# New places for operands and a second order of products in one feed-forward product of a two-layer encoder

## The chip, the cores and the metric

The kernel runs on one core of a Trainium2 chip. The metric is device time in microseconds (us) from the first to the last instruction of the program on the slowest core, here the only one. A core has five engines that run side by side: TensorE multiplies matrices (PE in the profile; PEld is its loading of the stationary operand), VectorE (DVE), ScalarE (ACT) and GpSimd (POOL) work elementwise, SyncE (SP) starts transfers. Tiles lie in SBUF, 128 partitions wide; products are summed in PSUM, eight banks of 512 float32 a partition.

## The reference

Two layers act on 272 tokens (16 learned meta tokens and 256 others) of width 2048. Each layer projects the tokens once, runs two groups of attention heads on the result (a gated linear attention in both directions, and a neighbourhood attention over a grid), joins them by an output projection, and then applies a feed-forward block of width 8192. After both, the residual stream is normalised. What the change touches is the second product of the feed-forward block:

```python
    ff = jnp.einsum('blf,fd->bld', jnp.square(jax.nn.relu(jnp.einsum('bld,df->blf', h, w_ff1))), w_ff2)
    return _layer_norm(DEEPNORM_ALPHA * h + ff, ln2_w, ln2_b)
```

The inner product and the squared ReLU give 272 x 8192 activations, which the kernel calls u; w_ff2 is 8192 x 2048. All is float32.

## The kernel before

**Split operands.** Every float32 operand is held as two rounded parts, a high and a low one (dtype float32r), and a product is the sum of three: high weights by high activations (h), high weights by low activations (l), low weights by high activations (w). The weights' parts are made on the chip: a block of 128 x 1024 weights is fetched into a tile `raw`, ScalarE rounds it to `wh` (L275, `rest`) and VectorE forms `wl = raw - wh` (L277). `made` does this one block after another in the order that the generator `order` yields, three blocks ahead of TensorE; four buffers each of `wh` and `wl`, 1280 floats wide, are in rotation, three of `raw`.

**Places.** A block of 1024 weights is eight blocks of 128, stored in pairs. `blocks`, `block` and `pairs` place them in the 1280 floats by three numbers, in floats: where the first block begins, the step from the first block of a pair to the second, the step from one pair to the next. The tables HIGHS and LOWS give these for each kind of block; for the stage of the change the kind is "all":

```python
"all": (0, P, 2 * P)                # HIGHS, P = 128
"all": (0, P + 16, 2 * P + 64)      # LOWS
```

Activations lie in chunks of 128 features by 272 tokens. `pair` makes one: a tile of 2 x 288 floats, the high part in the first 288, the low part in the second, so 1152 bytes apart and 2304 bytes in all. The inputs of a product are 16 such chunks (x, y), or 32 (y and u).

**Layer one's feed-forward block** (`tail`, with l = 0) goes over the 8192 features in two halves of 4096, that is 32 chunks: 16 take the tiles of y, which are free by then, and 16 are in a pool of their own, u. In each half the first product (w_ff1) writes the 32 chunks, and the second product (w_ff2) sums over them into the accumulator `acc` of 16 output chunks of 128 features each. The second product is `by_m`, called for groups g = 0 to 3 of four outputs m = 0 to 3: for each output, four groups of eight chunks (y 0 to 7, y 8 to 15, u 16 to 23, u 24 to 31), and for each group one call of `weights` and one of `eight`.

**`eight`** (L311) issues the 24 matmuls of a group into one PSUM bank: weights stationary (128 x 128), activations moving (128 x 272). Their order is a string, where each letter counts up its own chunks:

```python
TURNS = {True: "hwhwhwhwhwhwhwhw", False: "hlhlwwhlhlwwhlhlwwhlhlww"}
```

The second string is used where the moving operand is 272 wide. Each matmul loads its stationary operand anew. After each group `pump` lets a piece of other work be issued where some is waiting (in this stage hardly any; in half 1 the pieces of the layer norm), and after the last group of an output `ev_2` adds the bank to `acc` (L991, or `ln_part` in half 1). No planner is at work: the order of instructions is the order of the program, on each engine's own queue; the semaphores between engines are placed by the framework.

By the same line L311 run layer one's other by-output products; L363 is the same in another order of loops (`by_k`, the first product of a layer), L323 and L1184 are layer two's products, which have 256 tokens.

Of the kernel before, what the change touches and what calls it, by code (L numbers as in the profile page):

```python
# [8 lines left out]
F32R = mybir.dt.float32r  # L9
# [5 lines left out]
P = 128  # L15
D = 2048
DC = D // P
T = 256
NM = 16
L = T + NM  # L20
# [27 lines left out]
HIGHS = {"flat": (16, P, 2 * P), "once": (0, P, 2 * P), "two": (0, P, 2 * P), "all": (0, P, 2 * P), "all2": (0, P, 2 * P), "own2": (0, P + 48, 2 * P + 64)}  # L48
LOWS = {"flat": (16, P, 2 * P), "once": (16, P + 32, 2 * P + 64), "two": (16, P + 16, 2 * P + 64), "all": (0, P + 16, 2 * P + 64),
        "all2": (0, P + 48, 2 * P + 64), "own2": (0, P + 32, 2 * P + 64)}  # L50
TURNS = {True: "hwhwhwhwhwhwhwhw", False: "hlhlwwhlhlwwhlhlwwhlhlww"}


def plan(half, g):

    n, last = FEWER[half][g], HELD if half and g == 3 else 0
    special = list(range(FIRST, FIRST + n))
    plain = [k for k in range(DC) if k not in special]
    out = [(plain.pop(0), "flat")]
    for i, k in enumerate(special):  # L60
        out += [(k, "quad"), (plain.pop(0), "flat"), (k, "sums")]
        more = (i + 1) * (DC - 2 * n - 2 - last) // n - i * (DC - 2 * n - 2 - last) // n
        out += [(plain.pop(0), "flat") for _ in range(more)]
    return out + [(k, "flat") for k in plain]
# [13 lines left out]
class Trunk:  # L78
# [93 lines left out]
    def order(self):  # L172

        i, first = self.i, [(), (WB // 2, WB)]
        for l in range(DEPTH):
            last = l + 1 == DEPTH
            kind = lambda short, name: name if last and short else "all"
            na = [kind(c % 3 == 0, "two") for c in range(24)]
            groups = [(i["win"][l, g], [kind(g in (3, 4, 5), "two")] * 4 if g < 6 else na[4 * g - 24:4 * g - 20]) for g in range(12)]
            if last:  # L180
                groups[0] = groups[0][0], ["all2"] * 4
            groups += [(i["wout"][l, g], [kind(True, "once")] * 4) for g in range(4)]
            for half in range(2):
                groups += [(i["wff1"][l, 8 * half + g], [kind(True, "once") if half or g > 1 else ("all2", "own2")[last]] * 4)
                           for g in range(8)]
                groups += [(i["wff2"][l, half, g], plan(half, g) if last else ["all"] * 4) for g in range(4)]
            if l == 0:
                for t in range(groups[0][0].shape[0]):
                    for w, _ in groups[:2]:
                        yield w[t], first.pop(0) if first else (WB,), "all"  # L190
                groups = groups[2:]
            for w, kinds in groups:
                n = w.shape[0]
                if n == DC and last and isinstance(kinds[0], tuple):
                    for t, kind in kinds:
                        yield w[t], (WB,), kind
                    continue
                for t in range(n):
                    yield w[t], (WB,), kinds[4 * t // n]
# [94 lines left out]
        for at in (slice(4, 6), slice(6, 8)):  # L294
            self.halves(raw[:, at.start * P:at.stop * P], wh, wl, at)

    def eight(self, ps, wh, wl, x, n, first, last, once):

        mm = self.nc.tensor.matmul
        seen = dict.fromkeys("hlw", 0)
        for i, kind in enumerate(TURNS[once]):
            j = seen[kind]
            seen[kind] += 1
            w, v, o = wl if kind == "w" else wh, x[j], ps[:, :n]
            rhs = v[kind == "l"][:, :n]
            if once:
                rhs, o = (v.once, ps) if kind == "h" else (v[0][:, :T], ps[:, T:])  # L310
            mm(o, lhsT=self.block(w, j), rhs=rhs, start=first and not i, stop=last and i == len(TURNS[once]) - 1)  # L311

    def sixteen(self, ps, x, first, last, pump):

# [58 lines left out]
                self.nc.tensor.matmul(o, lhsT=self.block(both[low], i), rhs=rhs, start=not low and k + i % 2 == 0,  # L373
                                      stop=k == DC - 2 and i % 2 == 1 and not low, skip_group_check=True)

    def by_m(self, acts, ns, evict, pump=(0, 0), apart=False, renew=False, slim=()):

        nk = len(acts)
        for m, n in enumerate(ns):
            once = n == T and m not in slim  # L380
            ps = self.pm.tile([P, 512], F32, name="mm", tag="mm")
            step = 16 if once and acts[0].dense else 8
            for k in range(0, nk, step):
                if step > 8:
                    self.sixteen(ps, acts[k:k + 16], not k, k == nk - 16, pump)
                else:
                    wh, wl = self.weights()
                    self.eight(ps, wh, wl, acts[k:k + 8], n, not k, k == nk - 8, once)
                if k < nk - step:
                    self.pump(*pump)  # L390
                if renew and m == len(ns) - 1 and not k:
                    self.renew(2)
            parts = [ps[:, :T], ps[:, T:]] if once else [ps[:, :n]]
            evict(m, parts if apart else self.whole(parts))
            self.pump(*pump)
# [11 lines left out]
    def pair(self, pool, name, c):  # L407
        both = pool.tile([P, 2, PITCH], F32R, name=f"{name}{c}", tag=f"{name}{c}", bufs=1)
        return Pair(both, dense=name in ("y", "u") and not self.full)


    def layer(self, l):
        nc, tc = self.nc, self.tc
# [524 lines left out]
    def tail(self, ps):  # L938
        nc, tc, l, n = self.nc, self.tc, self.l, self.n
        last = l == DEPTH - 1  # L940
        acc = self.acc
        with tc.tile_pool(name="u", bufs=1, reuse_waits="tile") as up:
# [5 lines left out]
            for g in range(1, 4):  # L948
                self.by_m(self.y, [n] * 4, lambda m, ps: self.ln_part(4 * g + m, 0, ps),
                          pump=(0.75 if last else 1, 0), apart=True)  # L950
            self.fg.append(self.ln_norm(0, l, n))
            for half in range(2):
                u = [self.pair(self.yp, "y", k) if k < DC else self.pair(up, "u", k) for k in range(2 * DC)]
                if last:
                    u = [self.turned(x.both, k % 2) for k, x in enumerate(u)]
                    self.u, self.combined = u, {}
# [17 lines left out]
                for g in range(8):  # L974
                    if half or g > 2:
                        self.by_m(self.x, [n] * 4, lambda m, ps: ev_f(4 * g + m, ps), pump=(1, 0))
                    elif g == 2:
                        ps = self.by_k(self.x, n, self.normed, ends=True)
# [4 lines left out]
                    else:  # L983
                        self.by_m(self.x, [n + 2] * 4, lambda m, ps: self.fixed(ev_f, 4 * g + m, ps),
                                  pump=(1, NORMS[1]), renew=g == 1)

                def ev_2(m, ps, g):
                    k = 4 * g + m
                    a = acc[:, k, :n]
                    if half == 0:  # L990
                        nc.vector.scalar_tensor_tensor(a, a, ALPHA, ps[0], ALU.mult, ALU.add)  # L991
                        for part in ps[1:]:
                            nc.vector.tensor_tensor(a, a, part, ALU.add)
                    else:
                        self.ln_part(k, 1, ps)
# [3 lines left out]
                for g in range(4):  # L999
                    if last:  # L1000
                        self.across(u, half, g)
                    else:
                        self.by_m(u, [n] * 4, lambda m, ps: ev_2(m, ps, g), pump=(1, 0), apart=True)
            if last:
                self.lctx.close()
            else:
# [514 lines left out]
```

## Time and profile before

| | |
|---|---|
| median of 3 runs | 2309.95 us (2308.13 to 2310.82) |
| the profiled execution: time / span | 2308.73 / 2306.8 us |
| granted clock of TensorE | 0.997 |
| TensorE busy | 2290.6 us (99% of the span), 18289 matmuls |
| VectorE / ScalarE / GpSimd busy | 1658.0 / 1269.8 / 157.3 us |
| the second feed-forward product of layer one, half 0 / half 1 | 187.7 us from 623.9 / 188.2 us from 999.2 |

The span is the time from the first to the last instruction in the profile; the execution's own time is a little longer. A matmul's duration in the profile is its latency in a pipeline, so durations of consecutive matmuls overlap and their busy times can't be summed; the distance of two starts is what a matmul takes of TensorE's time. "x" counts instructions. A window's row gives for each engine the busy time within the window and the count of instructions that touch it.

### The profile page before, as it was taken

Reading aid. Unit: us, or ns where it says so; the run is one execution under the profiler, and the core shown is the slowest. Engines: PE = TensorE matmul, PEld = TensorE weight load, DVE = VectorE, ACT = ScalarE, POOL = GpSimd, SP = SyncE. Lnnn points to the kernel's source line nnn. Section 1 sums busy time; section 2 is a strip of 40 time slices with the busy share of each in tenths; the row PEclk is TensorE's granted clock in tenths of the full one; section 3 lists DMA queues with packets and bytes.
Section 4 is the critical chain, followed back from the end, with each engine's and each line's share of the span. In section 5 each row is a group of like instructions: output and inputs, shape, how many; then the busy total and the mean of one; then the engine's idle time right before and its main releaser. Section 6 shows DMA issues by size and latency. Waiting matters only on the chain.

```text
span 2306.8 us, 45387 instructions
## 1 busy us (share of the span) xinstructions
PE 2290.6 (99%) x18289; PEld 2173.1 (94%) x18289; DVE 1658.0 (72%) x2657; ACT 1269.8 (55%) x2187; POOL 157.3 (7%) x243
## 2 busy tenths in 40 slices
PE   9999999999999999999999999999999999999998
PEld 9999999999999999999999899989988888888886
DVE  5588778875544455547566788788887888686988
ACT  5666765564433344444456766655765555555453
POOL 0023220100000000000011122200100000000000
PEclk9999999999999999999999999999999999999999
DMA  8556665556556666665655556666665566666664
GB/s 261 161 162 189 196 201 172 174 175 182 181 179 181 181 177 182 180 179 180 178 182 160 181 170 211 203 195 192 187 192 186 192 207 201 194 193 207 191 210 155
DMA packets 129698, 431.33 MB, mean 187 GB/s; under 512 B 14824, under 2 KB 23528, under 8 KB 129488
## 3 DMA queue, kind: packets, MB, share of 16 engines
q1 hardware_dynamic: 126608, 421.23, 59.5%
q10 hardware_dynamic: 2880, 7.21, 0.8%
q8 instruction: 143, 2.34, 0.4%
q14 instruction: 67, 0.55, 0.1%
HBM read 419.99 MB, written 8.39 MB: 186 GB/s over the span
## 4 chain that ended last, share of the span: by engine, by line
PE 79%; DVE 3%; ACT 1%; issue 1%; DMA 1%; POOL 0%; DVEq 0%; ACTq 0%; SPq 0%; POOLq 0%
PE mm L311 45%; PE mm L323 15%; PE mm L1184 11%; PE bg L1184 3%; PE mm L363 1%; PE bg L363 1%; PE bg L373 1%; PE mm L373 1%; DVE wl L277 1%; ACT wh L275 1%; DMA raw<-in_wff 0%; DVE acc L1374 0%; PE bg L912 0%; ACT ns L817 0%; DMA grow<-in_norm 0%
## 5 line engine op out<-in xcount | busy, mean ns | idle before, releaser
L277 DVE TENSOR_TENSOR wl<-raw,wh 128x1024 fp32r<-128x1024 f32 (+2 forms) x770 | 925.7, 1206 | 479.5 <-ACT wh L275 442.9
L275 ACT CAST wh<-raw 128x1024 fp32r<-128x1024 f32 (+2 forms) x770 | 794.5, 1033 | 660.3 <-PE mm L311 355.1
L311 PE MATMUL mm<-x,wh 128*128 128x272 f32 (+3 forms) x4544 | 805.8, 294 | 0.0
L311 PEld LDWEIGHTS mm<-x,wh 128*128 128x128 f32 x4544 | 647.5, 188 | 15.3 <-DVE gtn L638 0.3
L311 PE MATMUL mm<-x,wl 128*128 128x272 f32 (+3 forms) x2432 | 520.1, 284 | 0.0
L311 PEld LDWEIGHTS mm<-x,wl 128*128 128x128 f32 x2432 | 390.9, 188 | 0.0
L311 PE MATMUL mm<-y,wh 128*128 128x272 f32 x1408 | 230.0, 285 | 0.0
L311 PEld LDWEIGHTS mm<-y,wh 128*128 128x128 f32 x1408 | 195.3, 188 | 0.0
L323 PE MATMUL mm<-x,wh 128*128 128x512 f32 x832 | 193.8, 390 | 0.0
L323 PEld LDWEIGHTS mm<-x,wh 128*128 128x128 f32 x832 | 154.3, 188 | 31.1
L311 PE MATMUL mm<-u,wh 128*128 128x272 f32 x1024 | 167.0, 285 | 0.0
L311 PE MATMUL mm<-y,wl 128*128 128x272 f32 x704 | 143.3, 285 | 0.0
L311 PEld LDWEIGHTS mm<-u,wh 128*128 128x128 f32 x1024 | 141.9, 188 | 0.0
L311 PEld LDWEIGHTS mm<-y,wl 128*128 128x128 f32 x704 | 110.1, 188 | 0.0
L1184 PE MATMUL mm<-wh,y 128*128 128x512 f32 (+1 forms) x448 | 109.2, 377 | 0.0
L311 PE MATMUL mm<-u,wl 128*128 128x272 f32 x512 | 104.2, 285 | 0.0
L323 PEld LDWEIGHTS mm<-x,wl 128*128 128x128 f32 x832 | 98.4, 188 | 2.0
L323 PE MATMUL mm<-x,wl 128*128 128x256 f32 x832 | 98.8, 276 | 0.0
L1184 PEld LDWEIGHTS mm<-wh,y 128*128 128x128 f32 x448 | 79.7, 188 | 14.1
L1184 PE MATMUL mm<-wh,u 128*128 128x512 f32 (+1 forms) x388 | 91.6, 356 | 0.0
L311 PEld LDWEIGHTS mm<-u,wl 128*128 128x128 f32 x512 | 80.0, 188 | 0.0
L1184 PEld LDWEIGHTS mm<-wh,u 128*128 128x128 f32 x388 | 68.7, 188 | 11.8
(339 smaller groups left out, 2797.4 us busy)
## 6 DMA issues: line engine op xcount, KB each, us to landing
raw<-in_wff SPq DMA_DIRECT2D x512, 512.0 KB, 3.6
raw<-in_win SPq DMA_DIRECT2D x190, 512.0 KB, 4.2
raw<-in_wout SPq DMA_DIRECT2D x64, 512.0 KB, 4.1
hop<-nt ACTq DMA_DIRECT2D x16, 384.0 KB, 2.3
np<-hop SPq DMA_DIRECT2D x64, 96.0 KB, 4.4
nb<-in_nab SPq DMA_DIRECT2D x16, 352.0 KB, 5.9
xraw<-in_xT SPq DMA_DIRECT2D x7, 272.0 KB, 5.4
grow<-in_norm SPq DMA_DIRECT2D x4, 256.0 KB, 5.5
```

Source lines behind the costliest of these rows:

```text
L275: self.nc.scalar.copy(h, r)
L277: self.wl = self.nc.vector.tensor_tensor(lo, r, h.bitcast(F32), ALU.subtract).ins
L311: mm(o, lhsT=self.block(w, j), rhs=rhs, start=first and not i, stop=last and i == len(TURNS[once]) - 1)
L323: self.nc.tensor.matmul(o, lhsT=self.block(both[j // 8][low], j % 8), rhs=rhs, start=first and not i + j, stop=bool(last and i and j == 15 ...
L363: self.nc.tensor.matmul(ps[g + m][:, :n], lhsT=self.block(parts[p][0], 4 * j + m if first else 2 * m + j), rhs=acts[k + j][parts[p][1]][:, ...
L373: self.nc.tensor.matmul(o, lhsT=self.block(both[low], i), rhs=rhs, start=not low and k + i % 2 == 0, stop=k == DC - 2 and i % 2 == 1 and n ...
L1184: nc.tensor.matmul(bank[to][:, at], lhsT=v, rhs=w, start=to not in begun, stop=stop, skip_group_check=True)
```

## The change

It touches layer one's second feed-forward product alone. The chunks u 16 to 31 get flat tiles in place of pairs, 592 floats wide up to 23 and 640 from 24 on, with other distances from the high to the low part, which differ between the halves. With y's pairs there are five kinds of places. The weight blocks get sixteen kinds, d0 to d15, one for each of the 16 outputs; a kind is a step between blocks and a beginning, in bytes, for the high and for the low weights. d12 is the old "all" for both. And the groups y 8 to 15, u 16 to 23 and, in half 0, u 24 to 31 take their 24 products in the order `hhhhllllwwww`, twice; the other groups keep the old order.

```diff
+FOURS = "hhhhllllwwww" * 2
+STEPS = {0: (P, 2 * P), 64: (P + 16, 2 * P + 32), 128: (P + 32, 2 * P + 64), 192: (624, P + 32)}
+DRAWS = [(0, r) for r in (0, 64, 128, 192)] + [(64, r) for r in (0, 64, 128, 192)] + [(128, 0), (128, 64), (192, 0), (192, 64)]
+DRAWS = [(d, d) for d in DRAWS] + [((0, 0), None), ((0, 0), (128, 0)), ((128, 64), (0, 0)), ((0, 32), (0, 32))]
+for i, d in enumerate(DRAWS):
+    for table, x in zip((HIGHS, LOWS), d):
+        table[f"d{i}"] = (x[1] // 4, *STEPS[x[0]]) if x else table["all"]
...
-                groups += [(i["wff2"][l, half, g], plan(half, g) if last else ["all"] * 4) for g in range(4)]
+                groups += [(i["wff2"][l, half, g], plan(half, g) if last else [f"d{4 * g + m}" for m in range(4)]) for g in range(4)]
...
-    def eight(self, ps, wh, wl, x, n, first, last, once):
+    def eight(self, ps, wh, wl, x, n, first, last, once, turns=None):
...
-        for i, kind in enumerate(TURNS[once]):
+        turns = turns or TURNS[once]
+        for i, kind in enumerate(turns):
...
-    def by_m(self, acts, ns, evict, pump=(0, 0), apart=False, renew=False, slim=()):
+    def by_m(self, acts, ns, evict, pump=(0, 0), apart=False, renew=False, slim=(), turns=(None,) * 4):
...
-                    self.eight(ps, wh, wl, acts[k:k + 8], n, not k, k == nk - 8, once)
+                    self.eight(ps, wh, wl, acts[k:k + 8], n, not k, k == nk - 8, once, turns[k // 8 % 4])
...
+    def places_of(self, pool, c, half):
+        if not self.full:
+            return self.pair(pool, "u", c)
+        wide = c >= 24
+        flat = pool.tile([P, 640 if wide else 592], F32R, name=f"u{c}", tag=f"u{c}", bufs=1)
+        at, low = 32 * (c % 2) if wide and half else 0, (272 if wide else 288) if half else 320
+        return flat[:, at:at + L], flat[:, at + low:at + low + L]
...
-                u = [self.pair(self.yp, "y", k) if k < DC else self.pair(up, "u", k) for k in range(2 * DC)]
+                u = [self.pair(self.yp, "y", k) if k < DC else self.places_of(up, k, half) for k in range(2 * DC)]
...
-                        self.by_m(u, [n] * 4, lambda m, ps: ev_2(m, ps, g), pump=(1, 0), apart=True)
+                        self.by_m(u, [n] * 4, lambda m, ps: ev_2(m, ps, g), pump=(1, 0), apart=True,
+                                  turns=(None, FOURS, FOURS, None if half else FOURS))
```

More of the change, by code (lines that the diff above doesn't have):

```diff
@@ L310, in eight @@
                 rhs, o = (v.once, ps) if kind == "h" else (v[0][:, :T], ps[:, T:])
-            mm(o, lhsT=self.block(w, j), rhs=rhs, start=first and not i, stop=last and i == len(TURNS[once]) - 1)
+            mm(o, lhsT=self.block(w, j), rhs=rhs, start=first and not i, stop=last and i == len(turns) - 1)
     def sixteen(self, ps, x, first, last, pump):
```

## The prediction

> **What bounds the kernel.** I read the page first: the engine shares, the clock row, the chain of waits. The chain is the work that ended last, followed back; its rows give shares of the span.
>
> ```profile
> span 2306.8 us, 45387 instructions
> PE 2290.6 (99%) x18289; PEld 2173.1 (94%) x18289; DVE 1658.0 (72%) x2657; ACT 1269.8 (55%) x2187; POOL 157.3 (7%) x243
> ...
> PEclk9999999999999999999999999999999999999999
> ...
> PE mm L311 45%; PE mm L323 15%; PE mm L1184 11%; PE bg L1184 3%; PE mm L363 1%; PE bg L363 1%; PE bg L373 1%; PE mm L373 1%; DVE wl L277 1%; ACT wh L275 1%; DMA raw<-in_wff 0%; DVE acc L1374 0%; PE bg L912 0%; ACT ns L817 0%; DMA grow<-in_norm 0%
> ```
>
> TensorE is the bound, at a full clock, and line 311 (the function `eight`, which the change touches) is 45% of the chain. Next come two views by stretch: layer one's second feed-forward product alone, line 311 only, and all engines in almost the same stretches.
>
> ```profile
> core 0: us, PE busy (x) PEld busy (x), PEclk, DMA share, GB/s
> 623.90:811.60 187.70, 187.70 (x1538) 187.70 (x1537) 1.00 0.60 180
> 999.20:1187.40 188.20, 187.95 (x1538) 187.79 (x1537) 1.00 0.61 183
> ```
>
> ```profile
> 624.00:811.00 187.00, 187.00 (x1532) 187.00 (x1532) 85.82 (x81) 67.35 (x66) 0.00 (x0) 1.00 0.60 181
> ...
> 999.00:1187.00 188.00, 187.98 (x1538) 187.76 (x1537) 109.52 (x157) 79.84 (x100) 0.62 (x5) 1.00 0.61 183
> ```
>
> The stage has 2 halves x 16 outputs x 4 groups of eight chunks x 24 products = 3072 matmuls (the code; the two that each window has above 1536 are neighbours cut by its edge or another line's work). 187.70 us / 1536 is 122.2 ns from one matmul's start to the next. TensorE never waits here, so nothing moves the end of this stage but that pitch: one nanosecond of it is 3.07 us of the kernel. A matmul's own "mean ns" (285) is latency, not pitch, and says nothing here; starts in the timeline do.
>
> **What the pitch depends on.** The timeline's first column is the start, its second the busy time, the last count the matmuls merged. First the present order in this stage, `hlhlww` (h: high weights by high activations; l: high weights by low activations; w: low weights by high activations), four h/l then two w:
>
> ```profile
> 625.17 0.65 PE L311 MATMUL mm<-y,wh 128*128 128x272 f32 x4
> 625.66 0.41 PE L311 MATMUL mm<-y,wl 128*128 128x272 f32 x2
> ...
> 631.04 0.65 PE L311 MATMUL mm<-u,wh 128*128 128x272 f32 x4
> ```
>
> From 625.17 to 631.04 are 48 matmuls: 122.3 ns, y and u alike. Second, 512- and 256-column matmuls of layer two in long runs:
>
> ```profile
> 1955.33 7.44 PE L323 MATMUL mm<-x,wh 128*128 128x512 f32 x32
> 1962.61 3.80 PE L323 MATMUL mm<-x,wl 128*128 128x256 f32 x32
> 1966.24 6.08 PE L323 MATMUL mm<-x,wh 128*128 128x512 f32 x26
> ```
>
> 7.28 us / 32 = 227.5 and 3.63 / 32 = 113.4 ns: both 0.443 to 0.444 ns a column. For 272 columns that makes 120.5 ns, which I take as the pitch without loss; today's loss is then 1.7 ns. Third, the only place where 272-column matmuls run in the changed kernel's manner, several of one kind in a row (layer one's first product, at the start):
>
> ```profile
> 8.80 2.17 PE L363 MATMUL bg<-x,wh 128*128 128x272 f32 x16
> 10.80 1.17 PE L363 MATMUL bg<-x,wl 128*128 128x272 f32 x8
> 11.80 2.19 PE L363 MATMUL mm<-x,wh 128*128 128x272 f32 x16
> 13.83 1.17 PE L363 MATMUL mm<-x,wl 128*128 128x272 f32 x8
> 14.84 0.66 PE L363 MATMUL bg<-x,wh 128*128 128x272 f32 x4
> 15.34 0.41 PE L363 MATMUL bg<-x,wl 128*128 128x272 f32 x2
> 15.59 0.67 PE L363 MATMUL bg<-x,wh 128*128 128x272 f32 x4
> 16.09 0.41 PE L363 MATMUL bg<-x,wl 128*128 128x272 f32 x2
> 16.34 0.65 PE L363 MATMUL bg<-x,wh 128*128 128x272 f32 x4
> ...
> 17.07 0.65 PE L363 MATMUL bg<-x,wh 128*128 128x272 f32 x4
> ```
>
> 11.80 to 14.84 holds 24: 126.7 ns, a loss of 6.2. Then the order becomes `hlhlww`, and the first two sixes still take 0.75 us each (125 ns) before the third takes 0.73 (122). So at one shape, on one engine, with no wait, the pitch lies anywhere from 120.5 to 126.7, and a change of order has an after-effect of some twelve matmuls. Fourth, layer two's second product, 256 columns, the same places of the operands twice:
>
> ```profile
> 1875.46 0.39 PE L1184 MATMUL mm<-wh,y 128*128 128x256 f32 x2
> ...
> 1877.84 2.00 PE L1184 MATMUL mm<-wh,y 128*128 128x512 f32 x8
> ```
>
> ```profile
> 2154.44 0.40 PE L1184 MATMUL bg<-wh,u 128*128 128x256 f32 x2
> ...
> 2155.51 1.78 PE L1184 MATMUL mm<-wh,u 128*128 128x512 f32 x7
> ```
>
> The first stretch has 21 matmuls in 2.38 us, 113.3 ns; the second nine in 1.07 us, 118.9 ns. By the code all have the moving operand on one place and the stationary ones alternating between two, so equal places can still run in a good and in a bad state, 5.6 ns apart.
>
> **The hypothesis for the sum.** The change's own tables count places in steps of 64 bytes modulo 256, four places. I suppose that the moving operand is read 64 bytes (16 columns) at a time through these four in turn: no loss when the next operand begins one place after the last one ended, a loss when it begins on the very place just read. 512 and 256 columns are a multiple of four steps, so operands that all begin on one place follow on, and those rows have no loss. 272 columns are 17 steps. In the 24 matmuls at 11.80 each begins where the last ended: 6.2 ns. In `hlhlww` on pairs (high at 0, low at 1152 bytes, two places on; a pair is 2304 bytes, nine times 256) four of six begin one place too far and two repeat the place: 2 x 6.2 / 6 = 2.1 against 1.7 seen, so the four cost about nothing. It fits three rows, and it was made from them; that is its weakness.
>
> **The change, part by part.** No instruction is added or removed: 24 products a chunk group, the same loads and casts. What changes is order and addresses; by group (768 matmuls each over both halves):
>
> - y 0 to 7: old order, pairs as before: loss 1.7, difference 0.
> - y 8 to 15: `hhhhllllwwww`. Within a run of four every operand repeats the last place; h to l and l to w are one too far; w to h repeats. Ten of twelve: 5.2 ns, +3.5 x 768 = +2.7 us.
> - u 16 to 23: same order, but a chunk is 592 floats, 2368 bytes, so each begins one place after the one before. In half 0 (low part 1280 bytes on, the same place) every operand follows on: loss 0, -1.7 x 384 = -0.65 us. In half 1 (low part two places on) two of twelve jump by two; no row prices that for 272 columns, 0 to 6.2, middle 3.1: 0.5 ns, -1.2 x 384 = -0.45 us.
> - u 24 to 31, half 0: same order, chunks of 640 floats, all parts on one place: all repeat, 6.2 ns, +4.5 x 384 = +1.7 us. Half 1: old order, with odd chunks two places on and low parts one place on: h, l, h, l, w follow on, two of six are one too far: 0, -0.65 us.
>
> Together +2.65 us. **After-effect of an order:** old order follows new once an output (half 0 at the next output's y 0, half 1 at u 24): 32 times 12 x (125 - 122.2) = 34 ns, +1.1 us; below, 0, if the new places settle at once.
>
> **The sixteen kinds of weight blocks** are drawn one for each output: blocks step by 0, 64, 128 or 192 bytes beyond 512 and begin at 0 to 192 bytes; four are special, one of them today's own, one beginning at 32 bytes. No row has these kinds at 272 columns. Bounds: relief of the 1.7 ns in y 0 to 7, -1.3 us; at worst the bad state's 5.6 ns on all that I put at 1.7 or less, 768 x 3.9 + 768 x 5.6 + 384 x 5.1 = +9.3 us. The nearest row, alternating weight places at 113.3 ns without loss, says 0, and I take 0.
>
> **What is hidden.** Casts write to other strides. Layer two's stretch with strided places in both tiles and the present one:
>
> ```profile
> L275 ACT CAST wh<-raw x15: 1033/1050/1055, 1603.1 to 1644.2; 128x1024 fp32r<-128x1024 f32 x15
> ```
>
> ```profile
> L275 ACT CAST wh<-raw x64: 1047/1047/1052, 623.7 to 808.5; 128x1024 fp32r<-128x1024 f32 x64
> ```
>
> ```profile
> L277 DVE TENSOR_TENSOR wl<-raw,wh x64: 1224/1226/1226, 624.8 to 809.5; 128x1024 fp32r<-128x1024 f32 x64
> ```
>
> 1050 against 1047 ns: nothing. A group lasts 24 x 122.2 = 2930 ns, so a cast could double under TensorE's cover; without that cover 64 x 1.0 us would show in each half. DMA is at 0.60 with unchanged bytes. u's pool grows by 8 x 64 + 8 x 256 = 2560 bytes a partition; its first u chunk is written well after attention's tiles are dead, so no new wait. No wait is added, and the new order asks for the low weights four matmuls later.
>
> **Sum.** 2.65 + 1.1 + 0 = +3.75 us. The profiled execution took 2308.73 us (span 2306.8 plus 1.9 around it), the median of three is 2309.95, 1.2 more. 2308.73 + 3.75 = 2312.5 for its like; **2313.7** for the median, +0.16%.
>
> **Pages weighed.** The Trainium skill's "SBUF — State Buffer", section "SBUF: two separate sides", says that PE never waits on another engine for SBUF, and lists a second, independent read port for LDWEIGHTS; by that, places would matter to nobody and the time would stay at 2309.95. The start's rows (126.7 against 122) show a dependence on order, though not yet on places. The Trainium skill's "TensorE: Matmul & The Clock Gate", section "Back-to-back issue gap", gives N / 2.4 + 2.5 ns, an estimate of 115.8 for 272 columns, which would leave 6.4 ns or 19.7 us to gain; the 512-column row here (227.5 against that page's 215.8) does not agree.
>
> **Rivals.**
>
> 1. *Places and order trade evenly*, as where a second state of the engine, not an address, sets the pitch (the two 256-column rows speak for it; the start's change of pitch with order against): 2310. Chance 0.2.
> 2. *Runs of four cost nothing*: the start's rows repeat the same activations for four outputs, while here each matmul has another chunk, and a pair is nine times 256, so neighbours differ by 256 bytes. If eight places count instead of four, nothing is repeated in y 8 to 15; leave them and u 24 to 31 at 1.7: -0.65 - 0.45 - 0.65 = -1.75, with the after-effect about 2309. Chance 0.17.
> 3. *The bad state holds in every run*, slower. Place: the 1920 matmuls in the new order. Price: 126.7 - 122.2 = 4.5 ns each, +8.6, with the after-effect +9.7: 2319.7. It decides (over 0.2%) once 4.6 / 0.0045 = 1020 of them run so. For it: the start's 24; against: rotating chunks exist only in the change. Chance 0.27.
> 4. *Loss vanishes everywhere*: -1.7 x 3072 = -5.2 us, 2304.7. Against: y 8 to 15 have no new places. With any gain below the 120.5 that no row shows: 0.07.
> 5. *It doesn't do what it says* (runs merged or places rounded away so that only noise is left): within rival 1.
>
> **How the numbers follow.** The forecast, 2311.5 to 2316, gets 0.29. About 0.2%, 4.6 us, is what a measurement of this kernel tells from no change. Slower than 2314.6: rival 3 and the upper part of the forecast, 0.27 + 0.12 = 0.39. Faster than 2305.3: rival 4 and a tail of rival 2, 0.08. Within: 0.53. The range, 2306.5 to 2320.5, leaves out rival 4 and the upper tail of the draws (+9.3 on top).
>
> **What would show it.** Half 0's stretch should take about 190.7 us for 187.7 and half 1's 189.0 for 188.2: half 0 is to bear the loss. In starts 24 matmuls apart: y 0 to 7 near 2.93 us, y 8 to 15 3.02, u 16 to 23 2.89, u 24 to 31 3.04 in half 0 and 2.89 in half 1. If y 8 to 15 stay at 2.93, rival 2 holds; if u 16 to 23 also stand at 3.04, rival 3. If outputs differ with the weights' kind more than groups do, the hypothesis on the moving operand was the wrong half of the story. Any idle time of TensorE at line 311, or other stages moved by over 1 us, would make the whole account wrong.

## The result and the profile after

The changed kernel takes 2319.11 us (median of three, 2318.32 to 2321.96) against 2309.95 (2308.13 to 2310.82): a ratio of 1.0046, 95% interval 1.0032 to 1.0059. It is slower by 9.2 us, where the forecast was +3.75; the time lies within the stated range, 2306.5 to 2320.5, near its upper end. The page of the changed kernel; `eight` is now L319, the rounding L282, the low weights L284:

```profile
span 2317.2 us, 45387 instructions
...
PE 2300.4 (99%) x18289; PEld 2182.4 (94%) x18289; DVE 1657.8 (72%) x2657; ACT 1269.6 (55%) x2187; POOL 157.5 (7%) x243
...
PEclk9999999999999999999999999999999999999999
...
L319 PE MATMUL mm<-y,wh 128*128 128x272 f32 x1408 | 222.5, 287 | 0.0
...
L319 PE MATMUL mm<-u,wh 128*128 128x272 f32 x1024 | 154.6, 288 | 0.0
```

The counts, the clock and the work of the other engines are as before; the span is 10.4 us longer and TensorE's busy time 9.8 us, with no idle time at line 319 (the last column). The last row misleads. Before, it was

```profile
L311 PE MATMUL mm<-u,wh 128*128 128x272 f32 x1024 | 167.0, 285 | 0.0
```

and so it seems to have become cheaper. But the busy time of a group of matmuls is the union of overlapping latencies: it depends on which kinds alternate and says nothing of what the group costs. The starts do. The stage alone, by stretch (line 319 only):

```profile
core 0: us, PE busy (x) PEld busy (x), PEclk, DMA share, GB/s
623.30:816.30 193.00, 193.00 (x1539) 193.00 (x1538) 1.00 0.59 175
1004.10:1197.20 193.10, 192.93 (x1539) 192.77 (x1538) 1.00 0.60 178
```

Before, the two halves took 187.7 and 188.2 us; now it is 193.0 and 193.1. That is +10.2 of the span's +10.4 (10.0 without the rounding of the windows' edges): the whole loss is in this stage, at a full clock, and the halves bear it alike, though their places and orders differ. 193.0 us / 1536 is 125.7 ns from start to start, for 122.2. Within one output (timeline; start, busy time, and at the end the matmuls merged; high and low weights appear as `wh` and `wl`):

```profile
635.38 0.66 PE L319 MATMUL mm<-y,wh 128*128 128x272 f32 x4
...
638.38 1.16 PE L319 MATMUL mm<-y,wh 128*128 128x272 f32 x8
...
641.37 1.16 PE L319 MATMUL mm<-u,wh 128*128 128x272 f32 x8
...
644.38 1.16 PE L319 MATMUL mm<-u,wh 128*128 128x272 f32 x8
...
647.35 0.29 PE L319 MATMUL mm<-y,wh 128*128 128x272 f32 x1
```

The four groups of 24 take 3.00, 2.99, 3.01 and 2.97 us, where 2.93 was usual. Even y 0 to 7, whose order and activations have not changed, lost. And the casts of half 0, all instructions that touch the two tiles of weights:

```profile
L282 ACT CAST wh<-raw x65: 1043/1048/1055, 623.3 to 816.0; 128x1024 fp32r<-128x1024 f32 x65
```

```profile
L284 DVE TENSOR_TENSOR wl<-raw,wh x64: 1224/1226/1227, 624.4 to 814.0; 128x1024 fp32r<-128x1024 f32 x64
```

1048 and 1226 ns at the median, for 1047 and 1226 before: the new strides cost the casts nothing.

### The profile page after: what moved, and what is told of

It is laid out like the page before. It is cut to its first block, busy times and chain, and to the rows that moved or that the text cites. A ratio compares the mean times of both kernels' runs of the same rounds, so it can differ in the third digit from the quotient of the medians.

```text
span 2317.2 us, 45387 instructions
## 1 busy us (share of the span) xinstructions
PE 2300.4 (99%) x18289; PEld 2182.4 (94%) x18289; DVE 1657.8 (72%) x2657; ACT 1269.6 (55%) x2187; POOL 157.5 (7%) x243
## 4 chain that ended last, share of the span: by engine, by line
PE 77%; DVE 4%; ACT 2%; issue 1%; DMA 1%; POOL 0%; DVEq 0%; ACTq 0%; SPq 0%; POOLq 0%
PE mm L319 43%; PE mm L331 15%; PE mm L1201 10%; PE bg L1201 3%; DVE wl L284 1%; PE bg L371 1%; PE mm L371 1%; PE bg L381 1%; PE mm L381 1%; ACT wh L282 1%; DMA raw<-in_win 0%; ACT ns L833 0%; DVE S L692 0%; DVE acc L1391 0%; PE bg L928 0%
## 5 line engine op out<-in xcount | busy, mean ns | idle before, releaser
L284 DVE TENSOR_TENSOR wl<-raw,wh 128x1024 fp32r<-128x1024 f32 (+2 forms) x770 | 926.2, 1207 | 480.2 <-ACT wh L282 436.5
L282 ACT CAST wh<-raw 128x1024 fp32r<-128x1024 f32 (+2 forms) x770 | 794.5, 1034 | 674.8 <-PE mm L319 379.9
L319 PE MATMUL mm<-x,wh 128*128 128x272 f32 (+3 forms) x4544 | 805.8, 294 | 0.0
L319 PEld LDWEIGHTS mm<-x,wh 128*128 128x128 f32 x4544 | 647.5, 188 | 15.3 <-issue 0.5
L319 PE MATMUL mm<-x,wl 128*128 128x272 f32 (+3 forms) x2432 | 519.9, 284 | 0.0
L319 PEld LDWEIGHTS mm<-x,wl 128*128 128x128 f32 x2432 | 391.0, 188 | 0.0
L319 PE MATMUL mm<-y,wh 128*128 128x272 f32 x1408 | 222.5, 287 | 0.0
L319 PEld LDWEIGHTS mm<-y,wh 128*128 128x128 f32 x1408 | 194.0, 188 | 0.0
L319 PE MATMUL mm<-u,wh 128*128 128x272 f32 x1024 | 154.6, 288 | 0.0
L319 PEld LDWEIGHTS mm<-u,wh 128*128 128x128 f32 x1024 | 138.6, 188 | 0.0
L319 PE MATMUL mm<-y,wl 128*128 128x272 f32 x704 | 134.6, 287 | 0.0
L319 PEld LDWEIGHTS mm<-y,wl 128*128 128x128 f32 x704 | 106.2, 188 | 0.0
L319 PE MATMUL mm<-u,wl 128*128 128x272 f32 x512 | 90.3, 288 | 0.0
L319 PEld LDWEIGHTS mm<-u,wl 128*128 128x128 f32 x512 | 74.3, 188 | 0.0
```

The source lines that it names most:

```text
L282: self.nc.scalar.copy(h, r)
L284: self.wl = self.nc.vector.tensor_tensor(lo, r, h.bitcast(F32), ALU.subtract).ins
```

## The experiments

Three theories stand in the expectations below. M is the prediction's hypothesis: only the moving operand's places count, with a gain for one that follows on. S says that the speed belongs to the whole repeating cycle of both operands' places (a cycle is the sequence of places that comes again and again, six matmuls long in the old order), and that after a change the engine needs some matmuls to settle into a steady speed. A says that each part of the change adds a share of its own. A place is a beginning modulo 256 bytes, counted in steps of 64 bytes; "settled" means without the first matmuls after a change.

The table collects the readings of the stage from the two kernels and from the six experiments that keep its products: the sum of both halves, each from its first start to the first start behind it, and the mean distance of two starts in each group of eight chunks, in half 0 and half 1, from the starts 24 apart of all 16 outputs (in output 4 of half 1 two matmuls of the layer norm fall where the first two groups meet, which adds 0.4 to 0.5 ns to their means). The kernels are named by what they contain of the change.

| kernel | stage, us | y 0 to 7 | y 8 to 15 | u 16 to 23 | u 24 to 31 |
|---|---|---|---|---|---|
| before | 376.0 | 122.2 / 122.7 | 122.2 / 122.6 | 122.2 / 122.2 | 122.2 / 122.2 |
| the whole change | 386.0 | 125.2 / 125.3 | 125.7 / 126.2 | 125.3 / 125.3 | 126.2 / 125.6 |
| new order alone (e1) | 384.9 | 124.2 / 122.7 | 125.9 / 126.3 | 126.1 / 126.1 | 126.1 / 124.3 |
| weights' kinds alone (e2) | 384.3 | 125.2 / 125.5 | 124.8 / 125.2 | 124.9 / 124.9 | 124.8 / 124.8 |
| u's places alone (e3) | 382.3 | 124.2 / 124.6 | 122.2 / 122.6 | 125.3 / 125.0 | 125.9 / 125.0 |
| kinds and places, old order (e4) | 385.0 | 125.0 / 125.3 | 124.8 / 125.2 | 125.3 / 125.3 | 125.6 / 125.4 |
| before, weights 64 B later (e7) | 384.9 | 125.5 / 125.0 | 125.6 / 125.1 | 125.6 / 124.7 | 125.5 / 124.7 |
| before, weights and activations 64 B later (e8) | 376.1 | 122.3 / 122.8 | 122.2 / 122.7 | 122.2 / 122.2 | 122.2 / 122.2 |

### One part at a time

The new order alone, from the changed kernel:

```diff
-                groups += [(i["wff2"][l, half, g], plan(half, g) if last else [f"d{4 * g + m}" for m in range(4)]) for g in range(4)]
+                groups += [(i["wff2"][l, half, g], plan(half, g) if last else ["all"] * 4) for g in range(4)]
...
-                u = [self.pair(self.yp, "y", k) if k < DC else self.places_of(up, k, half) for k in range(2 * DC)]
+                u = [self.pair(self.yp, "y", k) if k < DC else self.pair(up, "u", k) for k in range(2 * DC)]
```

> Only the order changes: u keeps its pairs and every block the old kind. Theory S (a settled state): the old stage repeats the same six steps 124 119 121 126 121 122 ns for 3072 matmuls because it has settled into a state that needs many equal sixes; any other order leaves it, costs about 125.6 ns a matmul wherever it runs, and spoils some 16 of the 24 old-order matmuls behind it. S expects the five groups in the new order at 125 to 126.5, the old-order group y 0 to 7 at 124.5 (not 122.2), the stage at 384 to 386.5 us for 375.9, that is the whole change's loss of 10. Theory M (the prediction's: moving operands that begin on the place just read cost 6.2 ns): y 8 to 15 at 125.7, both u groups in the new order too (pairs, so the same repeats), y 0 to 7 at 122.2 to 123.6, stage 382.5 to 383.5 us.

Measured 2320.12 against 2310.71 (one timing each), +9.4; the stage +8.9. The second output, by starts:

```profile
636.21 0.66 PE L319 MATMUL mm<-y,wh 128*128 128x272 f32 x4
...
636.97 0.66 PE L319 MATMUL mm<-y,wh 128*128 128x272 f32 x4
...
637.72 0.66 PE L319 MATMUL mm<-y,wh 128*128 128x272 f32 x4
...
638.46 0.65 PE L319 MATMUL mm<-y,wh 128*128 128x272 f32 x4
...
639.20 1.17 PE L319 MATMUL mm<-y,wh 128*128 128x272 f32 x8
...
642.22 1.18 PE L319 MATMUL mm<-u,wh 128*128 128x272 f32 x8
```

y 8 to 15 take 3.02 us, as forecast for this order on pairs. In y 0 to 7, back in the old order, the sixes take 0.76, 0.75, 0.74 and 0.74 us: the after-effect outlasts twelve matmuls, and the group's mean of 124.2 makes it 24 x 2.0 = 48 ns a change, not 34.

The weights' kinds alone, everything else as before:

```diff
-                u = [self.pair(self.yp, "y", k) if k < DC else self.places_of(up, k, half) for k in range(2 * DC)]
+                u = [self.pair(self.yp, "y", k) if k < DC else self.pair(up, "u", k) for k in range(2 * DC)]
...
-                                  turns=(None, FOURS, FOURS, None if half else FOURS))
+                                  turns=(None,) * 4)
```

> Only the sixteen kinds of weight blocks: old order, u in pairs. Theory S: the old steps return in output 12 alone (the old kind, 122.2 ns after some 16 matmuls); other kinds end in other repeating steps, or in none; between 122 and 126 by kind, mean about 124.5, stage 381 to 384 us. Theory M: weights' places do not enter, all outputs at 122.2, stage 376 us. A third, A (each part adds its own share of the 10.1 us): about 3 us, 379.

Measured 2317.56 against 2310.71, +6.9; the stage +8.3. The activations and the order are those of before, so nothing but the stationary operand's places can have done this: M falls. Each output ends in one VectorE row, the addition of its bank to `acc`; from one such row to the next are 96 matmuls. Outputs 10 to 13:

```profile
744.07 0.44 DVE L1007 SCALAR_TENSOR_TENSOR acc<-acc,mm 128x272 f32<-128x272 f32 x1 [0.93 <-PE mm L319]
...
756.11 0.44 DVE L1007 SCALAR_TENSOR_TENSOR acc<-acc,mm 128x272 f32<-128x272 f32 x1 [0.95 <-PE mm L319]
...
768.03 0.44 DVE L1007 SCALAR_TENSOR_TENSOR acc<-acc,mm 128x272 f32<-128x272 f32 x1 [0.91 <-PE mm L319]
...
779.80 0.44 DVE L1007 SCALAR_TENSOR_TENSOR acc<-acc,mm 128x272 f32<-128x272 f32 x1 [0.87 <-PE mm L319]
...
791.84 0.44 DVE L1007 SCALAR_TENSOR_TENSOR acc<-acc,mm 128x272 f32<-128x272 f32 x1 [0.96 <-PE mm L319]
```

12.04, 11.92, 11.77 and 12.04 us, or 125.4, 124.2, 122.6 and 125.4 ns. Output 12 is the old kind; the rest of its excess is the settling after output 11 (then it runs at 122.2). The kinds lie between 123.9 and 125.6 once settled, and all 15 others are dearer than the old one. Even d0, which differs from the old kind only in that low blocks step by 512 bytes and not alternately by 576, costs 124.4.

u's places alone:

```diff
-                groups += [(i["wff2"][l, half, g], plan(half, g) if last else [f"d{4 * g + m}" for m in range(4)]) for g in range(4)]
+                groups += [(i["wff2"][l, half, g], plan(half, g) if last else ["all"] * 4) for g in range(4)]
...
-                                  turns=(None, FOURS, FOURS, None if half else FOURS))
+                                  turns=(None,) * 4)
```

> Only u's five kinds of places: old order, old weight blocks. Theory S: y 0 to 15 at 122.2 once settled (y 0 to 7 about 123.5, since it follows u's group), u 16 to 23 and 24 to 31 at 124 to 126, stage 380 to 382 us. Theory M: u 16 to 23 repeats a place twice in six and jumps two once, 123.1; u 24 to 31 follows on in half 1, 120.5, and repeats four times in six in half 0, 124.7; stage about 376.5 us, half 1 faster than before. Theory A: about 379.

Measured 2316.88 against 2310.71, +6.2; the stage +6.3. The second output:

```profile
635.43 0.65 PE L319 MATMUL mm<-y,wh 128*128 128x272 f32 x4
...
638.41 0.65 PE L319 MATMUL mm<-y,wh 128*128 128x272 f32 x4
...
641.34 0.66 PE L319 MATMUL mm<-u,wh 128*128 128x272 f32 x4
...
644.35 0.67 PE L319 MATMUL mm<-u,wh 128*128 128x272 f32 x4
...
647.37 0.65 PE L319 MATMUL mm<-y,wh 128*128 128x272 f32 x4
```

2.98, 2.93, 3.01 and 3.02 us: the two groups with new places are dear, y 0 to 7 behind them pays the after-effect though its order never changed, and y 8 to 15 is free. So moved activations cost too: neither operand alone sets it.

All but the order:

```diff
-                                  turns=(None, FOURS, FOURS, None if half else FOURS))
+                                  turns=(None,) * 4)
```

> The change without its new order: draws and places, old order everywhere. Theory S: no settled steps anywhere but y of output 12, 125 to 125.7 ns, stage 384 to 386 us, as the whole change. Theory M: near e3, 376 to 377 us. Theory A: two thirds of the loss, 382 to 383.

Measured 2317.96 against 2310.71, +7.2; the stage +9.0. The parts don't add: +8.9, +8.3 and +6.3 alone, 23.5 together, where the whole change costs 10.0. Each part by itself takes the stage to a mean of 124.4 to 125.3 ns, and a second or third adds little to the dearest (125.3 for two, 125.7 for all). These four are single timings, so their order among each other by total time is not settled; the stage's stretches are. Against the expectations for the stage, M missed all four by 1.4 to 8.3 us and A the three that it priced by 2 to 5; S held for e1 and e4 and was 0.3 us short for e2 and e3.

### What the places do

Three probes replace the stage's products and compute something else: each output becomes 96 matmuls of the same shape, with high weights only, at chosen places. First, regular steps: the moving operand advances by a places of 64 bytes (modulo four) from one matmul to the next, the stationary by b; a = o // 4, b = o % 4 for output o. In half 1 the moving operand is also 256 bytes further on in every second matmul.

```diff
+            v, w = 16 * (o // 4 * i % 4) + (64 * (i % 2) if h else 0), 128 * (i % 7) + 16 * (o % 4 * i % 4)
+            self.nc.tensor.matmul(ps[:, :n], lhsT=wh[0](w, []), rhs=self.flat[:, v:v + n], start=not i, stop=i == end - 1)
```

> A measurement, not a candidate: layer one's second product is left out as a computation; in its place the same 3072 matmuls of 272 columns read u's first chunk and the high weights only, so the output is not the reference's. Each output has one regular pair of steps for its 96 matmuls: the moving operand's beginning goes on by a places of 64 bytes from one matmul to the next (a = output // 4), the stationary block's by b (b = output mod 4), both modulo four; in half 1 every second moving operand also lies 256 bytes further, as neighbouring chunks of y do. Theory M (moving operand alone): a = 1 follows on, 120.5 ns whatever b is; a = 0 repeats the place, 126.7; a = 2 near 120.5; a = 3 between. Theory S (the pitch belongs to the cycle of both operands together): for each a it differs with b by 2 ns or more, and no row of a is 120.5 throughout. Half 1 as half 0 if four places count; different if eight do.

The ends of outputs 2 to 4, 6 and 7:

```profile
657.41 0.44 DVE L1009 SCALAR_TENSOR_TENSOR acc<-acc,mm 128x272 f32<-128x272 f32 x1 [0.70 <-PE mm L318]
...
669.71 0.44 DVE L1009 SCALAR_TENSOR_TENSOR acc<-acc,mm 128x272 f32<-128x272 f32 x1 [0.77 <-PE mm L318]
...
681.71 0.44 DVE L1009 SCALAR_TENSOR_TENSOR acc<-acc,mm 128x272 f32<-128x272 f32 x1 [0.69 <-PE mm L318]
...
705.82 0.44 DVE L1009 SCALAR_TENSOR_TENSOR acc<-acc,mm 128x272 f32<-128x272 f32 x1 [0.69 <-PE mm L318]
...
717.66 0.44 DVE L1009 SCALAR_TENSOR_TENSOR acc<-acc,mm 128x272 f32<-128x272 f32 x1 [0.66 <-PE mm L318]
```

Output 3 (a = 0, b = 3) takes 12.30 us, 128.1 ns; output 4 (a = 1, b = 0: the moving operand follows on, which M put at 120.5) 12.00, 125.0; output 7 (a = 1, b = 3) 11.84, 123.3. All sixteen, settled, in ns:

| | b = 0 | 1 | 2 | 3 |
|---|---|---|---|---|
| a = 0 | 125.3 | 125.0 | 125.0 | 128.3 |
| 1 | 125.0 | 126.1 | 125.0 | 123.3 |
| 2 | 123.3 | 123.3 | 125.6 | 124.7 |
| 3 | 125.8 | 123.9 | 124.2 | 125.0 |

No row is constant, so the stationary operand's step counts at every step of the moving one. Half 1 gave the same to 0.1 ns: 256 bytes more change nothing, so four places it is for the moving operand; that much of the hypothesis stands. Following on is worth nothing here: the row a = 1 has no output at 120.5, and its mean, 124.9, is above that of a = 2.

Second, the old order's cycle of six with only the low blocks' two places and the low activations' place changed (two places on in half 0, as in the kernel before, one in half 1; the two low blocks begin at places o // 4 and o % 4):

```diff
+            v, w = 16 * ((2, 1)[h] if i % 6 in (1, 3) else 0), 128 * (2 * (i // 6 % 3) + (0, 0, 1, 1, 0, 1)[i % 6]) + 16 * (0, 0, 0, 0, o // 4, o % 4)[i % 6]
```

> A measurement like the one before, its output not the reference's: the same 3072 matmuls on u's first chunk and high weights, now with the places that the old order h l h l w w gives. High parts begin on place 0, low parts two places on in half 0 (as in a pair) and one place on in half 1; high weights begin on place 0; the low weights' blocks of a pair on places o // 4 and o mod 4. Output 1 of half 0 is the kernel before, address for address modulo 256. Theory S (the pitch is a property of the whole cycle of both operands' places, nothing else): output 1 of half 0 at 122.2 ns, the same six steps; its fifteen neighbours, which differ in one or two of six stationary places, anywhere from 120.5 to 127, most at 124 to 126. If something other than places made the old stage's 122.2 (its real chunks, its buffers), output 1 comes out elsewhere, near 125.

The ends of outputs 0 to 2 of half 0:

```profile
635.84 0.44 DVE L1009 SCALAR_TENSOR_TENSOR acc<-acc,mm 128x272 f32<-128x272 f32 x1 [0.64 <-PE mm L318]
...
647.63 0.44 DVE L1009 SCALAR_TENSOR_TENSOR acc<-acc,mm 128x272 f32<-128x272 f32 x1 [0.63 <-PE mm L318]
...
659.67 0.44 DVE L1009 SCALAR_TENSOR_TENSOR acc<-acc,mm 128x272 f32<-128x272 f32 x1 [0.71 <-PE mm L318]
```

Output 1 has the places of the kernel before: 11.79 us with its settling, and 122.2 ns once settled. The other 31 lie between 124.4 and 126.7. A change at one or two of the six places is enough to lose 2.2 to 4.5 ns.

Third, the old cycle shifted as a whole: in half 0 the moving operand by o // 4 places, the stationary by o % 4.

```diff
+            v, w = 16 * (((2 if h == 0 else o % 4) * (i % 6 in (1, 3)) + (0 if h else o // 4)) % 4), 128 * (2 * (i // 6 % 3) + (0, 0, 1, 1, 0, 1)[i % 6]) + 16 * (((0, 0, 0, 0, 0, 1)[i % 6] + o % 4) % 4 if not h else (0, 0, o // 4, o // 4, 0, 1)[i % 6])
```

> A measurement, its output not the reference's, built as the two before. Half 0: the old order's places, with all moving operands shifted by o // 4 places and all stationary blocks by o mod 4. If the pitch comes from both reads meeting (theory S, as a relation between the two), only the difference of the shifts counts: 122.2 ns in outputs 0, 5, 10 and 15, four values in all, each four times. If one of the operands alone mattered, a row or a column of the table would be constant; if absolute places mattered, sixteen unrelated values. Half 1: the old places, but with the odd high-weight block o // 4 places on and the low activation part o mod 4 places on: output 2 is the old cycle, 122.2; the others are a search for a better one, 120.5 the least that rows of other shapes allow, 124 to 126.5 expected.

Half 0's steady distances (the mean of the last 72 of 96) make a pattern:

| moving \ stationary shift | 0 | 1 | 2 | 3 |
|---|---|---|---|---|
| 0 | 122.3 | 125.5 | 124.5 | 124.5 |
| 1 | 124.5 | 122.3 | 125.5 | 124.5 |
| 2 | 124.5 | 124.4 | 122.3 | 125.5 |
| 3 | 124.5 | 124.5 | 124.5 | 122.3 |

Ends of outputs 4 to 6:

```profile
681.30 0.44 DVE L1009 SCALAR_TENSOR_TENSOR acc<-acc,mm 128x272 f32<-128x272 f32 x1 [0.68 <-PE mm L318]
...
693.07 0.44 DVE L1009 SCALAR_TENSOR_TENSOR acc<-acc,mm 128x272 f32<-128x272 f32 x1 [0.63 <-PE mm L318]
...
705.11 0.44 DVE L1009 SCALAR_TENSOR_TENSOR acc<-acc,mm 128x272 f32<-128x272 f32 x1 [0.70 <-PE mm L318]
```

Output 5 (both shifted by one) takes 11.77 us, output 6 (stationary one further) 12.04. The diagonal is good whatever the shift, and output 6 costs 3.2 ns more: what counts is where the two operands stand to one another. Not four values come out, as expected, but three, 122.3, 124.5 and 125.5, and one cell is out of line. Output 12 (moving 3, stationary 0) has the weights one place ahead too, modulo four, but not 125.5. Ends of outputs 10 to 12:

```profile
752.78 0.44 DVE L1009 SCALAR_TENSOR_TENSOR acc<-acc,mm 128x272 f32<-128x272 f32 x1 [0.63 <-PE mm L318]
...
764.83 0.44 DVE L1009 SCALAR_TENSOR_TENSOR acc<-acc,mm 128x272 f32<-128x272 f32 x1 [0.70 <-PE mm L318]
...
776.78 0.44 DVE L1009 SCALAR_TENSOR_TENSOR acc<-acc,mm 128x272 f32<-128x272 f32 x1 [0.68 <-PE mm L318]
```

Output 11 takes 12.05 us and output 12 11.95. By the single starts, the cells of one difference repeat the same six distances, each difference its own: the diagonal 124 119 121 126 121 122 ns, the three other cells one place ahead 124 125 128 121 128 127. Output 12 repeats 122 126 123 125 126 124, which comes back in e7 below: this difference has two steady speeds. Half 1, with other steps within the cycle, lay between 122.2 and 126.7, and only the old cycle itself reached 122.2.

### The same in the kernel

If that is so, the kernel before must lose all by moving its weights 64 bytes, and get it back by moving its activations as well. From the kernel before, weights alone, nothing else touched:

```diff
+HIGHS["next"], LOWS["next"] = (16, P, 2 * P), (16, P + 16, 2 * P + 64)
...
-                groups += [(i["wff2"][l, half, g], plan(half, g) if last else ["all"] * 4) for g in range(4)]
+                groups += [(i["wff2"][l, half, g], plan(half, g) if last else ["next"] * 4) for g in range(4)]
```

> A whole kernel, the one before with one edit: in layer one's second feed-forward product every weight block, high and low, begins 64 bytes later. Order, draws and activations as before. Theory S with the measured table (stationary places one on against the moving ones: 125.5 ns for 122.2): +3.3 x 3072 = +10.1 us, as much as the whole change, stage 386 us, kernel near 2320. Theory M (moving operand alone) and theory A (three shares, of which this is part of one): 0 to +3 us.

And with it:

```diff
+                if not last:
+                    u = [(x.both[:, 0, 16:], x.both[:, 1, 16:]) for x in u]
```

> The kernel before, with every weight block and every activation part of that product 64 bytes later. Theory S: only the difference counts, so the old six steps and 122.2 ns come back, stage 376 us, the time of before within 0.1%. If absolute places or the addresses' end counted, the loss of the run with the weights alone would stay in part, 2312 to 2320.

Weights alone: 2318.55 us (2317.48 to 2319.49) against 2309.09, ratio 1.0042, interval 1.0027 to 1.0057. Both: 2310.11 against 2309.09, ratio 1.0004, interval 0.9995 to 1.0014. The stage (line 312), first with the weights moved, then with both:

```profile
622.80:815.60 192.80, 192.80 (x1538) 192.80 (x1538) 1.00 0.59 175
1003.40:1195.40 192.00, 191.84 (x1538) 191.68 (x1537) 1.00 0.60 179
```

```profile
623.00:810.80 187.80, 187.80 (x1539) 187.80 (x1538) 1.00 0.61 180
998.50:1186.90 188.40, 188.15 (x1539) 187.99 (x1538) 1.00 0.60 183
```

One shift of 64 bytes costs about what the whole change costs (8.9 us of the stage for 10.0), and the same shift of the other operand undoes it. This is shown in the kernel and not only in a probe.

The first of the two has a second finding. In half 1 two matmuls of the layer norm fall into output 4 (timeline, weights moved):

```profile
1050.07 0.66 PE L312 MATMUL mm<-u,wh 128*128 128x272 f32 x4
...
1053.83 0.66 PE L312 MATMUL mm<-y,wh 128*128 128x272 f32 x4
...
1054.68 0.39 PE L1055 MATMUL bg<-sp,ones 128*128 128x272 f32 x1
...
1055.29 0.28 PE L1055 MATMUL bg<-sp,ones 128*128 128x272 f32 x1
...
1056.53 0.66 PE L312 MATMUL mm<-y,wh 128*128 128x272 f32 x4
...
1064.00 0.66 PE L312 MATMUL mm<-y,wh 128*128 128x272 f32 x4
```

Ahead of them 30 matmuls take 3.76 us, 125.3 ns; behind them 60 take 7.47, 124.5. Over outputs 1 to 3 the mean is 125.6 and over outputs 5 to 14 it is 124.4: the same places in the same order have two steady speeds, and a disturbance moved the engine from one to the other. The six distances behind it are 122 126 123 125 126 124 ns, those of output 12 in the shifted cycles. That is why the stage took 384.9 us and not the 386 expected.

### A search for better places

Thirty-two cycles, some random, some chosen, in five orders of h, l and w, one for each output of the two halves:

```diff
+            v, w = MV[slot][i % len(MV[slot])], WW[slot][i % len(WW[slot])]
```

> A measurement, its output not the reference's, built as the probes before: 32 other cycles of places for the two operands, in the orders h l h l w w (10), h l w h l w (8), h h l l w w (6), l h w w h l (4) and h h h h l l l l w w w w (4), places drawn at random but for six. Theory S: pitches from 122 to 128, mean near 125.2, whatever the order; a run of four of one kind is no worse than the others. Theory M: the order with runs of four at 125.7 and up, the others lower. One below 122.2 would make a faster kernel than both.

They lie between 123.9 and 128.8 ns, and the orders overlap: `hlhlww` 123.9 to 126.7, `hlwhlw` 124.4 to 125.6, `hhllww` 125.6 to 128.8, `lhwwhl` 124.4 to 126.7, `hhhhllllwwww` 125.0 to 126.7. Of some 110 cycles timed in this case at 272 columns none is below the old one's 122.2. No version came out of this that beats the kernel before.

## Why the prediction was wrong, and where it was right

**The bound and the unit: right.** TensorE never waits in the stage, the clock is full, and only the distance of two starts moves its end: the stage's loss is 386.0 - 376.0 = 10.0 us, 3.3 ns on each of 3072 distances, and the span's is 10.4. Casts, transfers and the pool's size cost nothing, as said; the rest of the span moved by 0.2 to 0.4 us. Of the three outcomes, "slower than 2314.6" came, which had a chance of 0.39; "within", at 0.53, was held likelier.

**The failed step** is the hypothesis for the sum: "I suppose that the moving operand is read 64 bytes (16 columns) at a time through these four in turn: no loss when the next operand begins one place after the last one ended". That 64 bytes modulo 256 matter holds, though not that 64 is the least that does: in e2 output 15 differs from output 0 only in weights that begin 32 bytes later, and settles at 125.6 ns for 124.4. That the moving operand alone decides does not hold: other places of the weights alone cost 8.3 us of the stage (e2) or 8.9 (e7), and where they stand to the activations is what counts (p3, e7, e8). It was fitted to rows that don't vary the stationary places on their own, so they couldn't speak against it.

**From it came the wrong terms.** "The sixteen kinds of weight blocks": "The nearest row, alternating weight places at 113.3 ns without loss, says 0, and I take 0." Measured alone: +8.3 us, near the stated upper bound of +9.3. The row taken was one of two 256-column rows with like places; the other, 118.9 ns, was as near, and only the good one entered the sum. u 16 to 23, put at 0 to 0.5 ns of loss because they follow on, -1.1 us in all: measured +3.1 ns a matmul, +2.4 us; u 24 to 31 in half 1, put at no loss, -0.65 us, with half of the after-effect (+0.55) on top: 125.6 ns, +1.3. And y 0 to 7, put at 0 with the other half of the after-effect: +3.0 ns in half 0 and +2.6 in half 1, +2.1 us. These three groups are 3.5, 1.4 and 1.6 us above their forecast and the other two 0.2 below it: together the 6.3 us between +3.75 and the stage's +10.0.

**Terms that held.** y 8 to 15 in the new order on pairs: 3.02 us for 24 forecast, 3.02 measured in e1 and in the mean of the changed kernel's half 0 (125.7 ns); that is luck as far as the runs show, since the hypothesis behind it fell, and p1's all-repeating output has 125.3 and not 126.7. u 24 to 31 in half 0: 3.04 forecast, 126.2 x 24 = 3.03 measured, with the same reserve. The after-effect exists and has the forecast's sign, at 48 ns for 34 in e1; in the changed kernel it can't be told from the weights' loss in the same groups.

**The signs that were named.** Half 0 was to bear the loss (190.7 against 189.0); both took 193. u 16 to 23 near 3.01 us spoke for rival 3, and its time, 2319.7, is 0.6 from the measured one. But its place was wrong: it put 4.5 ns on the 1920 matmuls in the new order, while 3.3 ns on average are lost on all 3072, and without the new order the loss is nearly the same (e4). "If outputs differ with the weights' kind more than groups do" came true, but faintly: in half 0 outputs lie between 124.7 and 126.2 ns and groups between 125.2 and 126.2. Only the kinds alone (e2) show it plainly, where output 12 runs at 122.2 once settled and all others at 123.9 or more.

**Pages weighed.** The Trainium skill's "SBUF — State Buffer", section "SBUF: two separate sides", gives the weight load a read port of its own, from which the prediction drew "places matter to nobody", 2309.95: e7 and e8, 8.4 us apart with not an instruction between them but for addresses, don't agree, and the measurement decides. The Trainium skill's "TensorE: Matmul & The Clock Gate", section "Back-to-back issue gap", gives a formula for a matmul by itself; the estimate from it, 115.8 ns for 272 columns, is not reached by any cycle here; the lowest is 122.2.

**What stays open** is the law itself: why the old cycle loses 1.7 ns against the longer matmuls' rate and most others 4 to 6, and what the engine carries over from one matmul to the next so that a cycle takes some twelve to twenty matmuls to settle and can settle in two ways. Open too is why the new order alone, the same addresses in another sequence, costs 8.9 us. That the weight loads and the moving reads meet at the four places is the reading that fits p3, e7 and e8; no run here sees the reads themselves.

## What to carry to other kernels

Before changing addresses for speed, vary each operand's place alone, by 64 bytes, in the stage itself: here that one run prices the whole mechanism, and a rule fitted to rows that vary both at once doesn't. Where a tuned cycle is already on the lowest of its speeds, any one change of order or place loses nearly all that there is to lose, so costs of several such edits are neither added nor averaged. And read the cost of matmuls in starts, never in a group's busy time, which here fell (u with high weights, 167.0 to 154.6 us) while the stage grew by 10.

## What was not expected of the hardware

- For 272-column float32r matmuls, each with its own 128 x 128 weight load, the distance of two starts depends on the difference between the two operands' places modulo 256 bytes, in steps of 64: in the old cycle 122.3 ns when both are shifted alike, 125.5 or 124.5 with the weights one place ahead, 124.5 with two or three. Over all cycles it ranged from 122.2 to 128.8.
- Distances are not spread evenly: cycles of six settle mostly at 122.2, 123.3, 124.4, 125.5 or 126.7, steps of about 1.1 ns a matmul, or 6.7 ns a cycle, and some halfway between (123.9, 125.0, 126.1).
- The same places in the same order ran at 125.6 and, after two foreign matmuls, at 124.4 for the rest of the half.
- After a change of order or of places a group of 24 costs 48 ns more, though its own order and places are old (half 0 of e1 and e3, 124.2 ns in y 0 to 7).
